# Weight tiles given up one at a time, and a longer warm-up, in a projection and attention kernel

## The chip, the core and the metric

The kernel runs on one core of a Trainium2 chip. The metric is device time in microseconds (us). The kernel before was run three times: 1155.35, 1155.54 and 1156.7 us, median 1155.54 us.

## What is computed

One layer with a normalisation, a projection to q, k, v and a gate, a two-dimensional neighbourhood attention, an output projection with a residual, and a last normalisation. Sizes: 2048 tokens (32 rows of 64 columns), model width 1024, 16 heads of 64; each query sees 8 rows by 16 columns of keys. Everything is float32.

```python
h = rmsnorm(x, norm_0)                      # (2048, 1024)
q, k, v, gate = split(h @ w_in_0, 4)        # w_in_0: (1024, 4096)
s = q k^T / 8 + rpb bias, masked to the 8 x 16 neighbourhood
o = softmax(s) v                            # per head
y = x + (o * silu(gate)) @ w_out_0          # w_out_0: (1024, 1024)
out = rmsnorm(y, norm_f)
```

## The kernel before

**Products in three terms.** To keep float32 accuracy, both operands of a projection are split into a high part of type fp32r and a low rest. Each product is three matmuls: high x high, high x low, low x high. ScalarE (ACT) makes the high part by a copy that rounds (`wh` at L197, `hh` at L175). VectorE (DVE) or GpSimd (POOL) makes the low part by a subtraction (`wl` at L198, `hl` at L176). Which of the two engines makes `wl` goes by the parity of weight unit and part, and POOL is used only after the second half-stage has begun (`state["half"] > 0`).

**Units and halves.** The input projection has 16 weight units of 256 columns: four each of q, k, v and gate. The tokens come in four groups of 512, two of them per phase `ph`. `halves` (L230 to L238) is the list of half-stages, each one kind of unit with one token group: first k, then q with token group 0, the same with group 1, then v with both groups, the gate with both, then the next heads. A q, k or gate half (`group`, L378) has two output groups `a`, each with eight steps `k` of three matmuls (L386, L388, L390), so 48 matmuls. A v half calls `group_v` (L394) four times, each eight steps of L402, L404, L406. The very first half is different: `first_groups` (L417) works on both output groups at once, step by step, with matmuls L425, L426 and L427.

**Items.** `items` is the list of all operands in the order of first use: ("w", (unit, phase), part) for a quarter of a weight unit, ("x", part, group) for the inputs, and squares and statistics for the normalisation. `load_item` (L133) issues the load of one on the SyncE queue (SP); `use_item` (L164) splits it. `consume` takes the next item if `may_use` allows it; it is called at fixed places between matmuls, and `need` forces it. So the program's order on every engine follows from when `may_use` first says yes. At least 32 items, and always five beyond the last used, are loaded ahead; raw tiles are few (pool `raw`, 6), so a load can also wait on SP until an earlier raw tile has been split.

**Weight tiles.** Split weights lie in the pool `wp` (10 buffers, so five pairs of `wh` and `wl`). A pair holds two of the four parts of a q, k or gate unit (four steps), or one part of two v units together (two steps). `may_use` (L272) counts the pairs that are live, and allows a new one up to five. A pair counts as live until the last half-stage of its unit is over (`last_use`, compared with `done_halves`).

**Around it.** After a group its PSUM bank is emptied by `evac` (L348) with DVE, ACT and POOL work, and the results are stored by SP. From half-stage 9 on, attention is interleaved with the projections: `normalise` (L562, POOL scales the exponentials `x`), `turns` (L579, transposes on PE), `scores` (L536) and `values` (L603), fed by a credit of projection matmuls; `feed` may run on a little if an item has just been used (`calm`). At the end `outputs` (L726) interleaves the output projection. All engines work in program order, SP's queue too.

**The start.** SP issues the load of `g0`, then in order: part 0 of the first weights, x parts 0 and 1, weight part 1, x parts 2 and 3, and so on. TensorE (PE) runs ten matmuls on a zero tile (L779, L780) ahead of the first real product.

Of the kernel before, what the change touches and what calls it, by code (L numbers as in the profile page):

```python
# [10 lines left out]
F32 = mybir.dt.float32  # L11
# [3 lines left out]
AF = mybir.ActivationFunctionType  # L15
OP = mybir.AluOpType
# [5 lines left out]
NK = D // 128  # L22
# [45 lines left out]
def build(ctx, tc, x, xt, wg, rpb, w_out, n0, nf, masks, out):  # L68
    nc = tc.nc
# [58 lines left out]
    hh, hl = {}, {}  # L128
    rb = {}
    raws, wh, wl, asked_at = {}, {}, {}, {}  # L130
    woh, wol = {}, {}

    def load_item(it):  # L133
        kind, a, b = it
        if kind in "trz":
            return
        if kind == "x" and b == 0:
            t = vp([128, 4, 128], F32, "land").rearrange("p g d -> p (g d)") if a < 6 else sp([128, 512], F32, "land")
        elif kind == "x" and b == 1 and a >= 4:
            t = kp([128, 960], F32, "land")[:, :512]  # L140
        elif it in items[12:16]:
            t = qp([128, 512], F32, "land")
        else:
            t = raw([128, 512], F32, "raw")
        raws[it] = t
        asked_at[it] = clock[0]
        if kind in "xs":
            nc.sync.dma_start(t, xt[a * 128:(a + 1) * 128, b * 512:(b + 1) * 512])
        elif kind == "w":
            u = a[0]  # L150
            nc.sync.dma_start(t.rearrange("p (k c) -> p k c", c=256), wg[u, :, 2 * b:2 * b + 2, :])
        else:
            nc.sync.dma_start(t, w_out[a * 128:(a + 1) * 128, b * 512:(b + 1) * 512])

# [9 lines left out]
    def use_item(it):  # L164
        kind, a, b = it
        state["event"] = clock[0]
        if kind == "t":
            return stats(b)
        if kind == "r":
            return spread_rstd(b)  # L170
        t = raws.pop(it)
        if kind == "x":
            h, l = xs([128, 512], F32R, "hh"), xs([128, 512], F32R, "hl")
            hh[a, b], hl[a, b] = h, l
            nc.scalar.activation(h, t, AF.Copy, scale=g0[:, a:a + 1])  # L175
            nc.vector.scalar_tensor_tensor(l, t, g0[:, a:a + 1], h.bitcast(F32), op0=OP.mult, op1=OP.subtract)  # L176
            if b < 2:
                raws["z", a, b] = t
        elif kind in "sz":
            square(a, t, b)  # L180
        elif kind == "w":
            t = t.rearrange("p (k c) -> p k c", c=256)
            u, ph = a
            if KINDS["v"] <= u < KINDS["g"]:
                a = u // 2 * 2, ph
                if u % 2 == 0:
                    wh[a, b] = wp([128, 2, 512], F32R, "wh")
                    wl[a, b] = wp([128, 2, 512], F32R, "wl")
                s = slice(u % 2 * 256, u % 2 * 256 + 256)
                h, l = wh[a, b][:, :, s], wl[a, b][:, :, s]  # L190
            else:
                if b % 2 == 0:
                    wh[a, b // 2] = wp([128, 4, 256], F32R, "wh")
                    wl[a, b // 2] = wp([128, 4, 256], F32R, "wl")
                s = slice(b % 2 * 2, b % 2 * 2 + 2)
                h, l = wh[a, b // 2][:, s], wl[a, b // 2][:, s]
            nc.scalar.activation(h, t, AF.Copy)  # L197
            (nc.gpsimd if (b + u) % 2 and state["half"] > 0 else nc.vector).tensor_tensor(l, t, h.bitcast(F32), OP.subtract)  # L198
        else:
            h, l = xs([128, 512], F32R, "woh"), xs([128, 512], F32R, "wol")  # L200
            woh[a, b], wol[a, b] = h, l
            nc.scalar.activation(h, t, AF.Copy)
            (nc.gpsimd if b else nc.vector).tensor_tensor(l, t, h.bitcast(F32), OP.subtract)
# [3 lines left out]
    def stats(c):  # L207
        acc = accs[c % 2]
        p = bank(16, "prt")
        for i in range(4):  # L210
            nc.tensor.matmul(p[:, i:i + 1], acc[:, i * 128:(i + 1) * 128], ones[:, :1], start=True, stop=True)
        m = tiny.tile([128, 8], F32, name="m")[:, :4]
        nc.vector.tensor_scalar(m, p[:, :4], 1.0 / D, EPS, op0=OP.mult, op1=OP.add)
        rsqrt(rt[:, 4 * c:4 * c + 4], m, 4)
        dg = dgs[c] = ev([128, 512], F32, "dg")
        for i in range(4):
            nc.vector.tensor_scalar(dg[:, i * 128:(i + 1) * 128], ident, rt[:, 4 * c + i:4 * c + i + 1], None,
                                    op0=OP.mult)

    def spread_rstd(c):  # L220
        p = bank(512, "prb")
        nc.tensor.matmul(p, ones, dgs.pop(c), start=True, stop=True)
        rb[c] = rbp([128, 512], F32, "rb")
        nc.scalar.activation(rb[c], p, AF.Copy)
# [14 lines left out]
    last_use = {}  # L239
# [10 lines left out]
    items, seen = [], set()  # L250
    for n, (k, j, ph, c) in enumerate(halves):
        a = (KINDS[k] + j, ph)
# [14 lines left out]
    items += [("o", a, b) for b in range(2) for a in range(NK)]  # L267
    AHEAD = 5
    clock = [0.0]
    state = dict(used=0, loaded=0, half=-1, done_halves=0, event=0.0)  # L270

    def may_use(it):  # L272
        kind, a, b = it
        d = state["done_halves"]
        if kind == "w":
            def tiles_(a, b):
                return (a[0] // 2 * 2, a[1], b) if KINDS["v"] <= a[0] < KINDS["g"] else (*a, b // 2)
            live = {tiles_(*i[1:]) for i in items[:state["used"]] if i[0] == "w" and last_use["w", i[1]] >= d}
            return len(live | {tiles_(a, b)}) <= 5
        if kind == "x":  # L280
            return sum(last_use["x", i] >= d for i in {i[2] for i in items[:state["used"]] if i[0] == "x"} - {b}) < 2
        if kind == "o":
            return last_use["x", 2 + b] < d
        return True
# [93 lines left out]
    def group(w, a, c, n):  # L378
        p = bank(512, "pp")
        cols = slice(a * 128, a * 128 + 128)  # L380
        for k in range(NK):
            if k in (3, 6) or n < 4:
                consume(1)
            need(("w", w, k // 2))
            need(("x", k, c))
            nc.tensor.matmul(p, wh[w, k // 4][:, k % 4, cols], hh[k, c], start=(k == 0), stop=False)  # L386
            yield 1
            nc.tensor.matmul(p, wh[w, k // 4][:, k % 4, cols], hl[k, c], start=False, stop=False)  # L388
            yield 1
            nc.tensor.matmul(p, wl[w, k // 4][:, k % 4, cols], hh[k, c], start=False, stop=(k == NK - 1))  # L390
            yield 1
        return p

    def group_v(w, t):  # L394
        c, o = divmod(t, 4)
        o = slice(o * 128, o * 128 + 128)
        p = bank(512, "pv")
        for k in range(NK):
            for u in range(2):
                need(("w", (w[0] + u, w[1]), k // 2))  # L400
            h, l = wh[w, k // 2][:, k % 2], wl[w, k // 2][:, k % 2]
            nc.tensor.matmul(p, hh[k, c][:, o], h, start=(k == 0), stop=False)  # L402
            yield 1
            nc.tensor.matmul(p, hh[k, c][:, o], l, start=False, stop=False)  # L404
            yield 1
            nc.tensor.matmul(p, hl[k, c][:, o], h, start=False, stop=(k == NK - 1))  # L406
            yield 1
            if k in (2, 5):
                consume(1)
        v = ev([128, 512], F32, "v")  # L410
        u = (w[0] - KINDS["v"]) // 2
        nc.scalar.activation(v, p, AF.Copy, scale=rt[:, t:t + 1])
        dst = vd[u].rearrange("h r c g d -> g (r c) h d")[t // 2, t % 2 * 128:t % 2 * 128 + 128]
        written.add(("v", u, t))
        store(("v", u, t), 8, lambda: nc.sync.dma_start(dst, v.rearrange("p (h d) -> p h d", h=4)))

    def first_groups(w):  # L417
        ps = [bank(512, "pp") for _ in range(2)]
        for k in range(NK):
            need(("x", k, 0))  # L420
            need(("w", w, k // 2))
            for a, p in enumerate(ps):
                cols = slice(a * 128, a * 128 + 128)
                h, l = wh[w, k // 4][:, k % 4, cols], wl[w, k // 4][:, k % 4, cols]
                nc.tensor.matmul(p, h, hh[k, 0], start=(k == 0), stop=False)  # L425
                nc.tensor.matmul(p, h, hl[k, 0], start=False, stop=False)  # L426
                nc.tensor.matmul(p, l, hh[k, 0], start=False, stop=(k == NK - 1))  # L427
        return ps

    def projections():  # L430
# [345 lines left out]
    z = ev([128, 512], BF16, "z")  # L776
    nc.gpsimd.memset(z, 0.0)
    zp = bank(512, "zp")
    for _ in range(10):  # L779
        nc.tensor.matmul(zp, z[:, :128], z, start=True, stop=True)  # L780

    amount = [96.0] * 16 + [(14 * 192 - 48 - 16 * 96) / 36] * 36 + [29.0] * 5 + [46.0] * 4 + [48.0] * (N + 1 - 61)
# [69 lines left out]
    for i in range(N + 1):  # L852
        a = amount[i]
# [52 lines left out]
```

## Time and profile before

| what | us |
|---|---|
| median of three runs | 1155.54 |
| the profiled execution | 1155.26 |
| its span, first to last instruction | 1153.5 |
| PE busy in the span | 1125.1 (98%) |
| DVE, ACT, POOL busy | 572.6, 467.5, 383.7 |
| projection matmuls L386, L388, L390, busy together | 885.5 |

A row of the timeline has start, duration, engine, line, operation, output and input tiles, and in brackets the idle time ahead of it and what ended it. A matmul's duration includes its way through the array, so consecutive starts, and not durations, give the pace. A row of the waits gives total, number and longest. A row of the windows gives, after the stretch and its length, the busy time of PE, of PE's weight loads, DVE, ACT and POOL with the number of instructions, then the granted PE clock, the DMA engines' share and GB/s.

### The profile page before, as it was taken

The page shows a single profiled execution, that of the slowest core. Times are in us where ns is not written, and L with a number is a line of the kernel's source. Part 1 is how long each engine was busy: PE and PEld are TensorE (multiplying, and loading weights), DVE is VectorE, ACT ScalarE, POOL GpSimd, SP SyncE. Part 2 cuts the span into 40 slices and gives each one's busy share as a digit, 9 for nine tenths or more (in the row PEclk, how much of TensorE's full clock was granted, in tenths as well). Part 3 has the DMA queues.
Part 4 walks back from the last instruction along what each step waited for, and adds up shares of the span by engine and source line. Part 5 has one row for each costly group of instructions (what it writes and reads, how often), then busy time and mean ns, then how long its engine had stood idle before and what let it go on. Part 6 is the DMA issues. An engine that isn't in the chain of part 4 may idle for free.

```text
span 1153.5 us, 21778 instructions
## 1 busy us (share of the span) xinstructions
PE 1125.1 (98%) x7858; PEld 916.4 (79%) x7858; DVE 572.6 (50%) x1453; ACT 467.5 (41%) x1190; POOL 383.7 (33%) x461
## 2 busy tenths in 40 slices
PE   8989999999999999999999999999999999999997
PEld 6868888888788888878887788888778777788875
DVE  6620554441244564126565455346555756566544
ACT  8222344232333444234444454344444544444322
POOL 1210442432232143314443544225533553233300
PEclk9999999999999999999999999999999999999999
DMA  7453867564554678457686787658877975865352
GB/s 244 126 160 109 270 213 219 162 225 110 154 183 145 214 222 240 118 165 195 224 245 198 207 250 222 208 163 230 235 230 210 281 230 188 255 194 189 104 174 73
DMA packets 139755, 224.45 MB, mean 195 GB/s; under 512 B 11776, under 2 KB 56320, under 8 KB 139648
## 3 DMA queue, kind: packets, MB, share of 16 engines
q1 hardware_dynamic: 139648, 223.06, 63.7%
q8 instruction: 62, 1.02, 0.4%
q14 instruction: 45, 0.37, 0.1%
HBM read 155.91 MB, written 67.11 MB: 193 GB/s over the span
## 4 chain that ended last, share of the span: by engine, by line
PE 58%; DMA 6%; DVE 3%; issue 3%; POOL 3%; ACT 1%; SPq 0%; DVEq 0%; POOLq 0%; ACTq 0%
PE pp L390 9%; PE pp L386 8%; PE pp L388 8%; PE o L617 6%; PE s L549 5%; PE po L763 4%; PE po L765 4%; PE po L761 4%; PE ph L572 3%; PE pv L404 3%; PE pv L402 3%; PE pv L406 3%; POOL x L567 1%; DMA ograw<-ogd 1%; DMA ogd<-og 1%
## 5 line engine op out<-in xcount | busy, mean ns | idle before, releaser
L390 PE MATMUL pp<-hh,wl 128*128 128x512 f32 x752 | 296.3, 394 | 2.0 <-POOL wl L198 2.0
L386 PE MATMUL pp<-hh,wh 128*128 128x512 f32 x752 | 295.3, 393 | 0.0
L388 PE MATMUL pp<-hl,wh 128*128 128x512 f32 x752 | 293.9, 391 | 0.0
L567 POOL TENSOR_SCALAR x<-x,st 128x360 f32<-128x360 f32 (+5 forms) x256 | 154.6, 623 | 250.7 <-DVE st L565 226.4
L559 ACT ACTIVATE x<-x,st 128x360 f32<-128x360 f32 (+5 forms) x256 | 151.8, 594 | 49.4 <-DVE st L556 49.3
L390 PEld LDWEIGHTS pp<-hh,wl 128*128 128x128 f32 x752 | 141.1, 188 | 33.4 <-POOL wl L198 2.9
L388 PEld LDWEIGHTS pp<-hl,wh 128*128 128x128 f32 x752 | 141.2, 188 | 30.5 <-issue 0.7
L386 PEld LDWEIGHTS pp<-hh,wh 128*128 128x128 f32 x752 | 141.2, 188 | 29.5 <-issue 0.5
L597 DVE COPY pta<-ph 128x384 f32<-128x384 f32 (+3 forms) x128 | 61.3, 516 | 165.8 <-PE ph L572 165.7
L198 POOL TENSOR_TENSOR wl<-raw,wh 128x512 fp32r<-128x512 f32 x60 | 83.3, 1393 | 161.6 <-ACT wh L197 155.2
L556 DVE CUSTOM_DVE_ANT_0 x<-s,em 128x360 f32<-128x360 f32 (+5 forms) x256 | 123.9, 539 | 7.3 <-PE s L549 5.3
L198 DVE TENSOR_TENSOR wl<-raw,wh 128x512 fp32r<-128x512 f32 x64 | 61.4, 969 | 93.9 <-ACT wh L197 92.6
L596 ACT ACTIVATE pta<-ph 96x256 f32<-96x256 f32 (+1 forms) x224 | 59.2, 333 | 118.7 <-PE ph L572 118.7
L402 PE MATMUL pv<-wh,hh 128*128 128x512 f32 x256 | 100.9, 394 | 3.5 <-ACT wh L197 3.5
L761 PE MATMUL po<-woh,gh 128*128 128x512 f32 x256 | 100.4, 392 | 2.1 <-ACT gh L671 2.0
L404 PE MATMUL pv<-wl,hh 128*128 128x512 f32 x256 | 101.4, 396 | 1.0 <-DVE wl L198 1.0
L763 PE MATMUL po<-woh,gl 128*128 128x512 f32 x256 | 100.4, 392 | 1.6 <-DVE gl L672 1.6
L765 PE MATMUL po<-wol,gh 128*128 128x512 f32 x256 | 100.9, 394 | 0.0
L406 PE MATMUL pv<-wh,hl 128*128 128x512 f32 x256 | 100.4, 392 | 0.0
L617 PEld LDWEIGHTS o<-pta,vt 96*64 96x64 f32 (+2 forms) x1792 | 83.8, 137 | 16.4 <-issue 11.0
L549 PE MATMUL s<-kt,qt 64*128 64x360 f32 (+5 forms) x768 | 93.1, 356 | 2.2 <-DVE pta L597 1.9
L531 POOL TENSOR_TENSOR em<-e,mk 128x360 f32<-128x360 f32 (+5 forms) x75 | 65.0, 869 | 89.9 <-DVE st L556 80.4
(85 smaller groups left out, 1373.9 us busy)
## 6 DMA issues: line engine op xcount, KB each, us to landing
raw<-in_wg_dram SPq DMA_DIRECT2D x124, 256.0 KB
vt<-vd SPq DMA_DIRECT2D x64, 192.0 KB
raw<-in_xt_dram SPq DMA_DIRECT2D x36, 256.0 KB
e<-in_rpb_dram SPq DMA_DIRECT2D x36, 240.0 KB
k_hi<-hi SPq DMA_DIRECT2D x32, 256.0 KB
k_lo<-lo SPq DMA_DIRECT2D x32, 256.0 KB
q_hi<-hi SPq DMA_DIRECT2D x32, 256.0 KB
q_lo<-lo SPq DMA_DIRECT2D x32, 256.0 KB
```

Source lines behind the costliest of these rows:

```text
L198: (nc.gpsimd if (b + u) % 2 and state["half"] > 0 else nc.vector).tensor_tensor(l, t, h.bitcast(F32), OP.subtract)
L386: nc.tensor.matmul(p, wh[w, k // 4][:, k % 4, cols], hh[k, c], start=(k == 0), stop=False)
L388: nc.tensor.matmul(p, wh[w, k // 4][:, k % 4, cols], hl[k, c], start=False, stop=False)
L390: nc.tensor.matmul(p, wl[w, k // 4][:, k % 4, cols], hh[k, c], start=False, stop=(k == NK - 1))
L404: nc.tensor.matmul(p, hh[k, c][:, o], l, start=False, stop=False)
L549: nc.tensor.matmul(pst[s], qq[a, qs], kk[a, :r1 - r0, c0:c1], start=(m == 0), stop=(m == 2))
L559: nc.scalar.activation(X[i, C][s], X[i, C][s], AF.Exp, bias=st[:, s:s + 1], scale=-1.0, accum_out=st[:, 2 + s:3 + s])
L567: nc.gpsimd.tensor_scalar(X[i, C][s], X[i, C][s], st[:, 4 + s:5 + s], 0.5, op0=OP.mult, op1=OP.mult)
L617: nc.tensor.matmul(o[s * 64:s * 64 + 64, C * 128 + q0:C * 128 + q0 + nq], vt[C][:k, g - g0_, s * 64:s * 64 + 64], t[:k, at:at + nq], start ...
L761: nc.tensor.matmul(p, gh[:, i], woh[i, j], start=(i == 0), stop=False)
L763: nc.tensor.matmul(p, gl[:, i], woh[i, j], start=False, stop=False)
L765: nc.tensor.matmul(p, gh[:, i], wol[i, j], start=False, stop=(i == NK - 1))
```

## The change

Three things are changed.

1. A weight pair stops counting as live when the program has written the last matmul that reads it, and not when its unit's last half-stage is over: `group` adds the pair to a set `freed` at steps 3 and 7 of the second output group of the unit's last half, `group_v` at every odd step of the last call in it, and `may_use` takes the set away from the live pairs.
2. 21 warming matmuls instead of ten.
3. In the first half, the three kinds of products go kind by kind: both output groups high x high, both high x low, both low x high. The first weight part is loaded as two halves, the second of them issued behind x part 0, and split in two as well, the second half behind x part 0's split.

```diff
+    second = []
...
         if kind in "xs":
             nc.sync.dma_start(t, xt[a * 128:(a + 1) * 128, b * 512:(b + 1) * 512])
+            if it == items[1]:
+                nc.sync.dma_start(raws[items[0]][:, 256:], wg[items[0][1][0], :, 1, :])
         elif kind == "w":
             u = a[0]
-            nc.sync.dma_start(t.rearrange("p (k c) -> p k c", c=256), wg[u, :, 2 * b:2 * b + 2, :])
+            if it == items[0]:
+                nc.sync.dma_start(t[:, :256], wg[u, :, 0, :])
+            else:
+                nc.sync.dma_start(t.rearrange("p (k c) -> p k c", c=256), wg[u, :, 2 * b:2 * b + 2, :])
...
+            if it == items[1]:
+                second.pop()()
...
-            nc.scalar.activation(h, t, AF.Copy)
-            (nc.gpsimd if (b + u) % 2 and state["half"] > 0 else nc.vector).tensor_tensor(l, t, h.bitcast(F32), OP.subtract)
+
+            def part(s, e):
+                nc.scalar.activation(h[:, s], t[:, s], AF.Copy)
+                e.tensor_tensor(l[:, s], t[:, s], h[:, s].bitcast(F32), OP.subtract)
+
+            if it == items[0]:
+                part(slice(0, 1), nc.vector)
+                second.append(lambda: part(slice(1, 2), nc.vector))
+            else:
+                part(slice(0, 2), nc.gpsimd if (b + u) % 2 and state["half"] > 0 else nc.vector)
...
+    freed = set()
...
-            live = {tiles_(*i[1:]) for i in items[:state["used"]] if i[0] == "w" and last_use["w", i[1]] >= d}
+            live = {tiles_(*i[1:]) for i in items[:state["used"]] if i[0] == "w" and last_use["w", i[1]] >= d} - freed
...
             nc.tensor.matmul(p, wl[w, k // 4][:, k % 4, cols], hh[k, c], start=False, stop=(k == NK - 1))
+            if k % 4 == 3 and a == 1 and n == last_use["w", w]:
+                freed.add((*w, k // 4))
...
             nc.tensor.matmul(p, hl[k, c][:, o], h, start=False, stop=(k == NK - 1))
+            if k % 2 and t % 4 == 3 and state["half"] == last_use["w", w]:
+                freed.add((*w, k // 2))
...
-            for a, p in enumerate(ps):
-                cols = slice(a * 128, a * 128 + 128)
-                h, l = wh[w, k // 4][:, k % 4, cols], wl[w, k // 4][:, k % 4, cols]
-                nc.tensor.matmul(p, h, hh[k, 0], start=(k == 0), stop=False)
-                nc.tensor.matmul(p, h, hl[k, 0], start=False, stop=False)
-                nc.tensor.matmul(p, l, hh[k, 0], start=False, stop=(k == NK - 1))
+            for m in range(3):
+                for a, p in enumerate(ps):
+                    cols = slice(a * 128, a * 128 + 128)
+                    t = (wl if m == 2 else wh)[w, k // 4][:, k % 4, cols]
+                    nc.tensor.matmul(p, t, (hl if m == 1 else hh)[k, 0], start=(k == 0 and m == 0),
+                                     stop=(k == NK - 1 and m == 2))
...
-    for _ in range(10):
+    for _ in range(21):
         nc.tensor.matmul(zp, z[:, :128], z, start=True, stop=True)
```

## The prediction

> **What bounds the kernel now.** I read the page first, then who waited for whom on TensorE, then the timeline at those places.
>
> ```profile
> span 1153.5 us, 21778 instructions
> PE 1125.1 (98%) x7858; PEld 916.4 (79%) x7858; DVE 572.6 (50%) x1453; ACT 467.5 (41%) x1190; POOL 383.7 (33%) x461
> PE pv L402 <- ACT wh L197: 3.5, 1, 3.5
> PE ph L572 <- POOL x L567: 3.2, 12, 0.4
> PE pp L425 <- ACT hh L175: 2.3, 1, 2.3
> PE pp L390 <- POOL wl L198: 2.0, 2, 1.0
> ...
> PE pv L404 <- DVE wl L198: 1.0, 1, 1.0
> ...
> PE pp L426 <- DVE hl L176: 0.3, 1, 0.3
> ```
>
> PE is busy 98% of the span, no other engine over 50%. So the time is PE's work at PE's pace, plus the few places where PE stands still or runs slowly. The number and kinds of real products do not change here, so only those places can move. Three kinds concern split weights or the start: L425 (2.3 us), L402 with L404 (4.5 us, one place), and L390 (2.0 us, two places).
>
> The pace, and the two slow places:
>
> ```profile
> 7.91 0.50 PE L425 MATMUL pp<-hh,wh 128*128 128x512 f32 x1 [2.27 <-ACT hh L175]
> ...
> 20.87 0.39 PE L386 MATMUL pp<-hh,wh 128*128 128x512 f32 x1
> ...
> 21.55 0.39 PE L386 MATMUL pp<-hh,wh 128*128 128x512 f32 x1
> 61.10 0.39 PE L406 MATMUL pv<-wh,hl 128*128 128x512 f32 x1
> ...
> 67.41 0.63 PE L402 MATMUL pv<-wh,hh 128*128 128x512 f32 x1
> 67.84 0.63 PE L404 MATMUL pv<-wl,hh 128*128 128x512 f32 x1
> ...
> 70.09 0.39 PE L404 MATMUL pv<-wl,hh 128*128 128x512 f32 x1
> 8.00:9.00 1.00, 0.72 (x2) 0.40 (x3) 1.00 (x2) 1.00 (x2) 0.00 (x0) 0.64 1.04 381
> 11.00:12.00 1.00, 1.00 (x4) 0.83 (x3) 1.00 (x3) 0.95 (x3) 0.00 (x0) 0.66 1.05 391
> ```
>
> Three matmuls take 21.55 - 20.87 = 0.68 us, so 0.227 us each at the full clock. From 67.41 to 67.84 it is 0.43: the granted clock is at half after an idle stretch. At the start it falls at about 8.3 us (0.64 over the slice 8 to 9) and is back at about 11.3 (0.66 over 11 to 12).
>
> **The start: 21 warming matmuls, order by kind, half loads.** The first 48 real products run from 7.91 to 20.87, 12.96 us, where 48 x 0.227 = 10.90 would do: 2.06 us lost, nearly all to the half clock.
>
> ```profile
> 1.83 3.81 PE L780 MATMUL zp<-z 128*128 128x512 bf16 x10 [1.83 <-POOL z L777]
> 4.37 0.15 PEld L780 LDWEIGHTS <-z 128*128 128x128 bf16 x1 [0.28 <-issue]
> 4.79 0.35 PEld L780 LDWEIGHTS <-z 128*128 128x128 bf16 x2 [0.28 <-issue]
> 8.42 0.63 ACT L197 ACTIVATE wh<-raw 128x512 fp32r<-128x512 f32 x1
> ...
> 10.44 0.63 ACT L197 ACTIVATE wh<-raw 128x512 fp32r<-128x512 f32 x1
> ```
>
> The weight loads of the warming matmuls are 0.43 us apart up to 4.79; the two at 4.79 lie within 0.35 us, so the second came 0.35 - 0.15 = 0.20 after the first. The clock was thus granted at about 4.8 us, lay unused from 5.64, and was taken back at 8.3. With 21, seven cold steps lead to 4.8 and fourteen more at about 0.214 (half of 0.427, an estimate) end at about 7.8. The first x part is split by 7.91 at the latest, so PE goes over into real products without a gap and keeps the clock. The eleven added matmuls cost nothing as long as PE would only wait; if that cover is gone, 0.1 to 1.6 us (below). Ordering by kind puts two products ahead of the first that needs `hl`; the wait of L426, 0.3 us, stood at that place, I keep 0.2. ACT delivers two steps in 10.44 - 8.42 = 2.02 us, PE consumes them in 12 x 0.227 = 2.72, so the extra load and the two half splits are hidden behind PE after the first step; the smaller first load can bring x sooner, but PE is then still warming, so that earns at most 0.1. New end of the first half: 7.85 + 10.90 + 0.2 = 18.95, **gain 1.9 us**. Bounds: 2.1 if nothing is left over, and below:
>
> Nothing says that the grant comes at 4.8 in every execution. If it came as late as the other edge shown, 8.3, the 21 would take 15 cold steps of 0.427 and 6 warm ones, ending at about 9.5; the first half would end at 9.5 + 10.9 = 20.4 and the gain be 0.4 us. That is the lower bound. [...]
>
> **The stall at 61 us: weight pairs given up one by one.** From 61.10 to 70.09 there are 11 steps, which take 8.99 us and should take 11 x 0.227 = 2.50. So this one place costs **6.49 us**: 4.5 idle, the rest half clock.
>
> ```profile
> 54.25 1.23 ACT L197 ACTIVATE wh<-raw 128x512 fp32r<-128x512 f32 x2 [2.89 <-DMA raw<-in_wg_dram]
> ...
> 63.76 0.61 ACT L197 ACTIVATE wh<-raw 128x512 fp32r<-128x512 f32 x1
> 48.25 1.98 SPq L151 DMA_DIRECT2D raw<-in_wg_dram  x3
> 53.72 0.33 SPq L151 DMA_DIRECT2D raw<-in_wg_dram  x1
> 55.55 1.28 POOL L198 TENSOR_TENSOR wl<-raw,wh 128x512 fp32r<-128x512 f32 x1 [4.76 <-ACT wh L197]
> ```
>
> The first two v units need four pairs. In q's last half q still holds two and v three, and a sixth is refused. So the split of v's last part (steps 6 and 7) was written only after the last q group, and stood on ACT behind the whole emptying of four banks, up to 63.76. In the changed program q's first pair is given up at step 3 of q's last output group. In the built order the split of the two quarters stands 13 and 19 products earlier, ahead of that emptying. All times here in the old frame: 61.10 is v's 18th product, so PE passes that step 3 some 30 products earlier, by 54.3. The loads of the two quarters were the last of the three issued from 48.25 to 50.23, and the one at 53.72. The slowest load near here, issued at 48.25, was used at 54.25, 6.0 us later; this gives at the latest 56.2 and 59.7. ACT is free from 55.48, and a split takes it 0.61. So `wh` is ready by 56.8 and 60.3 at worst, `wl` at most 1.3 us later: 58.1 and 61.6. PE wants them at 61.33 (step 6). If the second load takes half as long as the slowest (an estimate), there are 2.7 us to spare; at the worst 0.3 us are missing. The bank emptying moves behind at most one late load; its banks are wanted again only after groups of 24 x 0.227 = 5.4 us. I take **6.5 us**; bounds 0.3 us less if the worst load is late, 6.5 less if it doesn't work.
>
> **The gate after v: 2 x 1.0 us.** Here the reason is the same:
>
> ```profile
> 307.87 2.02 POOL L567 TENSOR_SCALAR x<-x,st 128x264 f32<-128x264 f32 x4 [31.86 <-DVE st L565]
> 309.86 2.52 POOL L198 TENSOR_TENSOR wl<-raw,wh 128x512 fp32r<-128x512 f32 x2
> 309.77 0.39 PE L388 MATMUL pp<-hl,wh 128*128 128x512 f32 x1
> 311.18 0.50 PE L390 MATMUL pp<-hh,wl 128*128 128x512 f32 x1 [1.02 <-POOL wl L198]
> ...
> 312.47 0.39 PE L388 MATMUL pp<-hl,wh 128*128 128x512 f32 x1
> 514.26 0.50 PE L390 MATMUL pp<-hh,wl 128*128 128x512 f32 x1 [1.02 <-POOL wl L198]
> ```
>
> The gate's third and fourth quarters need the pair of v's part 0, which was given up only when v was over. They are split when v is over; POOL has first to scale four `x` (2.02 us), and `wl` is late at step 6. From 309.77 to 312.47 six steps take 2.70 instead of 1.36: 1.34 us. The row at 514.26 shows the same wait, so 2.7 together. In the built order these splits stand 15 products, 3.4 us, earlier, ahead of POOL's `x`. That exceeds the delay, so **2.7 us** go; bounds 0 to 2.7.
>
> **Everything else that moves.** All other weight splits stand 6 to 18 products earlier (a few 30 to 46, past an attention block), with the loads that follow them; from the output weights on, the order is the same. A split waits on ACT for the matmul written just ahead of it; what stands behind it there needs later matmuls anyway, so this wait costs nothing. Attention blocks shift by at most a dozen products, with equal work. In three short attention intervals (22, 29, 32) a POOL split newly stands ahead of the scaling of `x`. I cost this at 0; the waits of L572 in the first fence show that the margin is small, bounded by 3 x 1.26 (two POOL splits take 2.52 above):
>
> ```profile
> 960.00:962.00 2.00, 1.64 (x18) 1.41 (x18) 0.82 (x2) 0.89 (x4) 0.42 (x1) 0.65 0.88 326
> 962.00:964.00 2.00, 2.00 (x16) 1.54 (x14) 1.34 (x5) 0.64 (x2) 0.00 (x0) 0.50 0.27 104
> ```
>
> The last two rows are a third half-clock stretch, by short attention waits: 1.4 + 2 us at half the clock, so up to 1.7 us lost. Moving everything by 11 us may keep it, drop it or make another: 1.7 either way.
>
> **Sum.** 1.9 + 6.5 + 2.7 = 11.1 us. The profiled execution took 1155.26 (1.76 around its span), so 1144.2; the median of the runs is 0.28 higher, so **1144.4 us**.
>
> **The rivals.**
>
> - *The stall moves* (9%). The last v quarters come just too late, because the second load can't be issued until its raw tile is split (53.72). The rest remains: 1144.4 + 6.5 = 1150.9. For it: ACT waited 2.89 us for a load there; against: at the worst 0.3 us are missing.
> - *The grant comes late* (8%): the start gains 0.4 instead of 1.9, so 1145.9, as worked out above from the two edges shown. For it: nothing ties the grant to the kernel's start; against: the one execution shown had it at 4.8. [...]
> - *Attention pays* (5%). The three POOL splits delay `turns` by 1.26 us each: 1148.2.
> - *Slower* (4%). SP works in order, and more than a dozen weight loads now stand ahead of attention's `vt` loads and of stores, each waiting for a raw tile (the first row is of 560 to 900 us):
>
> ```profile
> SPq L151 <- POOL wl L198: 6.8, 4, 3.5
> 306.84 0.55 SPq L507 DMA_DIRECT2D vt<-vd  x1
> 323.39 1.33 PE L617 MATMUL o<-pta,vt 96*64 96x128 f32 x24
> ```
>
>  A wait of 3.5 us at the head of SP, if it reached PE, would cost 3.5 per attention pair; from four such pairs on the gain is gone, and at five it is 1144.4 + 17.5 = 1161.9. Against it: a `vt` issued at 306.84 is used at 323.39 or later, a lead of over 16 us.
> - *Only the warm-up works* (4%): pairs come free earlier in the program, but PE waits at the same places: 1155.5 - 1.9 = 1153.6.
>
> **How the numbers follow.** The forecast has 70%. Its own range is 1142.5 (1.7 for the half clock, 0.2 at the start) to about 1146. The range of 8 in 10 reaches on over the late grant and attention's waits, to 1149; left out are 9 + 4 + 4 = 17%. A change of 0.2%, 2.3 us, is about what a measurement of this kernel can tell from none. Forecast, moved stall, late grant and attention lie under 1153.2: 92% faster; only the warm-up: 4% the same; 4% slower.
>
> **What would show it.** Right: in the profile after, no wait of L402 for `wh` and no slice under full clock between 60 and 70 us; the waits of L390 gone; the warming matmuls end at about 7.8 and the first L386 starts near 19.0. Wrong: a wait of `pv` for `wl` or of ACT for a weight load at 50 to 60 us (the stall moved); a gap or half clock between warming and the first products; more than 3.2 us of L572 waiting for `x`; `o` waiting for `vt`.

## The result, and the profile after

The median of four runs of the changed kernel is 1143.94 us (1142.6 to 1145.46), beside 1156.1 us for four runs of the kernel before. The ratio is 0.9898, 95% interval 0.9883 to 0.9913, so 10.0 to 13.5 us less; predicted was 1144.4. The profiled execution of after took 1145.46 us, the slowest of its four, against 1155.26 for that of before: 9.8 us less.

The first view is the head of the page after and its two longest waits (total us, number, longest):

```profile
span 1143.7 us, 21798 instructions
PE 1124.3 (98%) x7869; PEld 917.7 (80%) x7869; DVE 568.9 (50%) x1454; ACT 469.4 (41%) x1191; POOL 383.9 (34%) x461
PE po L782 <- ACT gh L692: 4.8, 2, 4.3
PE ph L593 <- POOL x L588: 2.8, 10, 0.4
```

The lines that the prediction was about are gone: no product of `pv` waits for `wh` or `wl` (before: 3.5 and 1.0 us), and no `pp` waits for POOL's `wl` (before 2.0). The scaling of `x` costs 2.8, not more than the 3.2 of before. New at the top is a wait of an output product for `gh`, 4.8 us, which stood in no step of the prediction. Eleven matmuls more, each with its weight load, are the warming; one instruction more on DVE and one on ACT are the halved first split.

Next, the same stretch of the windows in both kernels, before first, then after:

```profile
60.00:70.00 10.00, 5.57 (x17) 3.98 (x16) 4.99 (x5) 3.83 (x7) 3.32 (x3) 0.83 0.91 275
```

```profile
60.00:70.00 10.00, 10.00 (x46) 8.28 (x45) 4.66 (x6) 4.64 (x8) 3.90 (x3) 1.00 0.89 271
```

PE has 46 matmuls where it had 17, at a granted clock of 1.00 instead of 0.83.

The timeline of after, at the start and where v begins:

```profile
1.83 7.66 PE L801 MATMUL zp<-z 128*128 128x512 bf16 x21 [1.83 <-POOL z L798]
6.15 0.72 ACT L181 ACTIVATE hh<-land,g 128x512 fp32r<-128x512 f32 x1 [2.17 <-DMA land<-in_xt_dram]
9.13 0.82 PE L447 MATMUL pp<-hh,wh 128*128 128x512 f32 x2
20.23 0.39 PE L403 MATMUL pp<-hh,wh 128*128 128x512 f32 x1
54.81 2.66 ACT L207 ACTIVATE wh<-raw 128x512 fp32r<-128x512 f32 x4 [4.01 <-DMA raw<-in_wg_dram]
56.15 0.80 PE L421 MATMUL pv<-wh,hh 128*128 128x512 f32 x1
57.37 0.58 ACT L240 ACTIVATE rb<-prb 128x512 f32<-128x512 f32 x1
57.49 1.71 DVE L208 TENSOR_TENSOR wl<-raw,wh 128x512 fp32r<-128x512 f32 x1 [1.33 <-ACT wh L207]
```

The last four of v's eight splits now stand in one row on ACT, from 54.81, and the bank emptying (`rb`) comes behind them. The first real product starts at 9.13, behind the warming matmuls, which the prediction had end at about 7.8. Meanwhile x part 0 is split by 6.15 + 0.72 = 6.87, an us earlier than in before, and lies there waiting for PE.

Five places that both kernels pass in the same order say where the 9.8 us of the profiled executions went (us from the span's start, by the first matmul of each):

| place | before | after | difference |
|---|---|---|---|
| first half over | 20.87 | 20.23 | 0.64 |
| v begins | 56.79 | 56.15 | 0.64 |
| the gate behind the second v pair begins | 305.47 | 298.27 | 7.20 |
| the gate behind the third begins | 508.55 | 500.00 | 8.55 |
| last output product | 1145.23 | 1135.27 | 9.96 |

So the start gave 0.64, the stall 6.56, the first gate wait 1.35, and all that follows 1.41, in which the second gate wait (1.34) lies.

The last stretch holds more than that, and it cancels: without that gate wait it is 0.07 us shorter. The half-clock stretch of before at 961 is gone, but after has two others: one from 895.3 to 898.7 and one from 973.8 on, behind a wait for `gh` (each of them is the 0.97 in one row of 50 us below; before has 1.00, 1.00 and 0.97 in the same three). Timeline, windows and queue waits of after:

```profile
973.41 1.15 ACT L692 ACTIVATE gh<-ograw 128x512 fp32r<-128x512 f32 x2 [7.60 <-DMA ograw<-ogd]
974.09 0.80 PE L782 MATMUL po<-woh,gh 128*128 128x512 f32 x1 [4.33 <-ACT gh L692]
```

```profile
850.00:900.00 50.00, 48.81 (x436) 39.81 (x433) 33.36 (x87) 25.34 (x72) 14.61 (x22) 0.97 0.80 249
900.00:950.00 50.00, 48.77 (x425) 39.44 (x424) 33.28 (x82) 26.93 (x74) 29.96 (x33) 1.00 0.77 227
950.00:1000.00 50.00, 45.67 (x372) 36.78 (x371) 29.86 (x98) 21.50 (x62) 13.83 (x18) 0.97 0.71 220
974.00:975.00 1.00, 0.91 (x2) 0.47 (x3) 0.93 (x2) 0.56 (x2) 0.00 (x0) 0.50 1.05 350
```

```profile
SPq L680 <- DMA ogd<-og: 5.2, 1, 5.2
```

The first stretch follows a gap of 1.19 us on PE, which ends at 894.07. Before has the like gap ahead of the same products, 1.22 us up to 905.47, and keeps the full clock; from the end of the gap to the same product after it takes 1.56 us longer (4.81 instead of 3.25). At 974 PE stands for 4.33 us until ACT has split a tile of the attention's output, and resumes at half the clock. ACT waited for its load, and on SP's queue that load had waited 5.2 us for the store of the same data. In before's profile the store was waited for 2.5 us, and PE 1.70:

```profile
SPq L659 <- DMA ogd<-og: 2.5, 1, 2.5
984.87 0.49 PE L761 MATMUL po<-woh,gh 128*128 128x512 f32 x1 [1.70 <-ACT gh L671]
```

Shorter waits stand against this, among them those for `pta` and `gl` (1.9 and 1.6 us in before, 1.2 and 0.2 in after); the parts of this stretch were not all added up.

### The profile page after: what moved, and what is told of

It reads as the page before. It is cut to its first block, busy times and chain, and to the rows that moved or that the text cites. A ratio compares the mean times of both kernels' runs of the same rounds, so it can differ in the third digit from the quotient of the medians.

```text
span 1143.7 us, 21798 instructions
## 1 busy us (share of the span) xinstructions
PE 1124.3 (98%) x7869; PEld 917.7 (80%) x7869; DVE 568.9 (50%) x1454; ACT 469.4 (41%) x1191; POOL 383.9 (34%) x461
## 3 DMA queue, kind: packets, MB, share of 16 engines
q8 instruction: 62, 1.02, 0.4%
## 4 chain that ended last, share of the span: by engine, by line
PE 93%; DMA 2%; DVE 2%; POOL 1%; issue 1%; ACT 1%; DVEq 0%; SPq 0%; POOLq 0%; ACTq 0%
PE pp L407 15%; PE pp L405 15%; PE pp L403 15%; PE o L638 7%; PE s L570 6%; PE pv L423 5%; PE pv L425 5%; PE pv L421 5%; PE po L786 4%; PE po L784 4%; PE po L782 4%; PE ph L593 4%; PE pp L447 1%; POOL x L588 1%; DMA ograw<-ogd 1%
## 5 line engine op out<-in xcount | busy, mean ns | idle before, releaser
L407 PE MATMUL pp<-hh,wl 128*128 128x512 f32 x752 | 296.1, 394 | 0.0
L407 PEld LDWEIGHTS pp<-hh,wl 128*128 128x128 f32 x752 | 141.4, 188 | 30.3
L208 POOL TENSOR_TENSOR wl<-raw,wh 128x512 fp32r<-128x512 f32 x60 | 79.7, 1332 | 228.9 <-ACT wh L207 222.1
L552 POOL TENSOR_TENSOR em<-e,mk 128x360 f32<-128x360 f32 (+5 forms) x75 | 67.8, 905 | 102.5 <-DVE st L577 95.8
L208 DVE TENSOR_TENSOR wl<-raw,wh 128x512 fp32r<-128x512 f32 (+1 forms) x65 | 60.1, 928 | 79.5 <-ACT wh L207 78.3
L638 PEld LDWEIGHTS o<-pta,vt 96*64 96x64 f32 (+2 forms) x1792 | 84.3, 138 | 16.2 <-issue 11.3
L638 PE MATMUL o<-pta,vt 128*64 128x128 f32 (+4 forms) x1792 | 93.2, 255 | 0.5 <-DVE pta L618 0.5
```

The source lines that it names most:

```text
L638: nc.tensor.matmul(o[s * 64:s * 64 + 64, C * 128 + q0:C * 128 + q0 + nq], vt[C][:k, g - g0_, s * 64:s * 64 + 64], t[:k, at:at + nq], start ...
```

## The experiments

The theory is the prediction's: the stall of L402 and the waits of L390 come from where the splits stand on ACT and POOL, and giving pairs up early moves them ahead of what delayed them; the start gains what the clock grant allows. The main rivals: the gain is the warm-up's, or the moved splits pay elsewhere. Ratios are to the kernel before, with 95% intervals; its median stood at 1155.23, 1155.58 and 1155.31 us beside the three groups of experiments. The kernel line numbers shift by a few from kernel to kernel.

### e1_freed_only: only the giving up

Before, with the `freed` set in `may_use`, `group` and `group_v`, and nothing else of the change:

```diff
+    freed = set()
-            live = {... if i[0] == "w" and last_use["w", i[1]] >= d}
+            live = {... if i[0] == "w" and last_use["w", i[1]] >= d} - freed
+            if k % 4 == 3 and a == 1 and n == last_use["w", w]:
+                freed.add((*w, k // 4))
+            if k % 2 and t % 4 == 3 and state["half"] == last_use["w", w]:
+                freed.add((*w, k // 2))
```

> The kernel before with weight pairs given up at their last product, and nothing else: ten warming matmuls, old order and one whole first weight load. My theory: the stall at 61 us (6.5 us) and the two waits of L390 (2.7 us) go, the start stays, so 9.2 us less, ratio about 0.992; in the profile the first matmul of the second half stage (L386 of before) starts at 20.9 us as before. Rival (the start carries the gain, the pairs only move waits): less than 4 us gained, with new waits for weights elsewhere. Rival (the parts help each other): under 8 us, because the late start brings back part of the stall.

Measured: 1144.51 us, ratio 0.9915 (0.9903 to 0.9927), 9.8 us less. Its timeline and its waits:

```profile
20.90 0.39 PE L387 MATMUL pp<-hh,wh 128*128 128x512 f32 x1
```

```profile
PE po L766 <- ACT gh L676: 2.3, 2, 2.1
PE pp L430 <- ACT hh L175: 2.1, 1, 2.1
```

The first half ends where before's does (20.87), and the waits of `pv` and L391 are gone. The gates begin at 299.02 and 500.78: 6.45 and 7.77 earlier. Nearly the whole gain is this part's.

### e2_start_only: only the start

After, without the two `freed.add`:

```diff
-            if k % 4 == 3 and a == 1 and n == last_use["w", w]:
-                freed.add((*w, k // 4))
-            if k % 2 and t % 4 == 3 and state["half"] == last_use["w", w]:
-                freed.add((*w, k // 2))
```

> The changed kernel without giving up pairs: 21 warming matmuls, products by kind and the halved first load stay. My theory: 0.4 to 1.9 us gained by when the clock is granted, ratio 0.9984 to 0.9997; the wait of the v group for its weights near 60 us (3.5 and 1.0 us) and both 1.0 us waits for the gate's low parts stand as before, a little earlier. Rival (the start carries the gain): 4 us or more.

Measured: 1154.21 us over 12 runs, ratio 0.9996 (0.9986 to 1.0007): nothing that can be told from none. In the profile the start works and its gain is lost 45 us later. Timeline, waits and windows:

```profile
1.83 6.79 PE L797 MATMUL zp<-z 128*128 128x512 bf16 x21 [1.83 <-POOL z L794]
19.38 0.39 PE L403 MATMUL pp<-hh,wh 128*128 128x512 f32 x1
```

```profile
PE pv L419 <- ACT wh L207: 3.7, 1, 3.7
PE pv L421 <- DVE wl L208: 1.0, 1, 1.0
```

```profile
64.00:65.00 1.00, 0.25 (x1) 0.00 (x0) 1.00 (x2) 0.21 (x1) 0.52 (x1) 0.55 0.94 227
67.00:68.00 1.00, 1.00 (x4) 0.75 (x3) 0.00 (x0) 0.22 (x1) 0.00 (x0) 0.50 1.05 299
70.00:71.00 1.00, 1.00 (x4) 0.76 (x3) 0.00 (x0) 0.00 (x0) 0.34 (x1) 0.53 1.16 256
```

The first half ends 1.49 us earlier and v begins 1.49 earlier, at 55.30; the gate begins at 305.40, only 0.07 earlier. The wait of 3.7 + 1.0 is much that of before (3.5 + 1.0): it moved forward with PE and ends 1.21 earlier. But the half clock now lasts from 64.1 to 70.9, 6.8 us, where before's lasted from 66.3 to 69.7, 3.4 us. The two rows of before:

```profile
66.00:67.00 1.00, 0.58 (x2) 0.51 (x3) 0.87 (x2) 0.00 (x0) 0.00 (x0) 0.65 0.99 260
69.00:70.00 1.00, 1.00 (x4) 0.77 (x4) 0.00 (x0) 1.00 (x2) 0.00 (x0) 0.65 0.91 307
```

So in this execution the early start was lost to a longer half clock behind the stall, and only 0.3 us of it to a longer wait.

### e3_freed_qkg and e4_freed_v: the giving up in two parts

Before with `freed`, once added to only in `group` (q, k, gate), once only in `group_v`:

```diff
+            if k % 4 == 3 and a == 1 and n == last_use["w", w]:
+                freed.add((*w, k // 4))
```

> The kernel before, with pairs given up early only in the groups of q, k and gate. My theory: the stall at 61 us goes and both waits of L390 of 1.0 us stay: 6.5 us less, ratio about 0.9944. Rival (a general relief of ACT, POOL and the loads): about half of the 9.2 us with each half of the edit, and no clean assignment of waits.

```diff
+            if k % 2 and t % 4 == 3 and state["half"] == last_use["w", w]:
+                freed.add((*w, k // 2))
```

> The kernel before, with pairs given up early only in the groups of v. My theory: the stall at 61 us stays whole (waits of 3.5 and 1.0 us and half clock to 69.9) and both waits of L390 go: 2.7 us less, ratio about 0.9977. Rival (a general relief): about half of 9.2 us.

Measured: e3 1146.44 us, 0.9929 (0.9915 to 0.9943), 8.2 us less (6.6 to 9.8); e4 1154.17 us, 0.9986 (0.9976 to 0.9995), 1.6 less (0.6 to 2.8). The windows and waits of e3, then the waits of e4:

```profile
60.00:70.00 10.00, 10.00 (x46) 8.29 (x45) 5.54 (x6) 4.42 (x8) 4.08 (x3) 1.00 0.87 284
```

```profile
PE pp L391 <- POOL wl L198: 2.0, 2, 1.0
```

```profile
PE pv L403 <- ACT wh L197: 3.5, 1, 3.5
```

The two places part cleanly: `group`'s pairs carry the stall of v, `group_v`'s pairs the waits of the gate. By the places, e3 has gained 6.35 us at the third gate (502.20 against 508.55), e4 1.51 (507.04), of which 0.16 is its start. The medians lie 1.7 above (e3) and 1.1 below (e4) the 6.5 and 2.7 of the working; both intervals take in or nearly touch them, and the stretch behind the third gate, whose length varies from run to run (633.7 to 636.7 us in the twelve profiles that feed as before does there), can make that difference.

### e11_split_before_emptying: what the stall's cause is

Is it that the pair is free, or where the split stands on ACT? Before, without `freed`; only, at the end of q's last half, the two v quarters are split ahead of the last bank emptying instead of behind it:

```diff
                     if n == 3 and a == 1:
+                        state["done_halves"] = 4
+                        consume(2)
                         flush(1)
```

> The kernel before, except that the two last v quarters are split right after the last q product, ahead of the emptying of the four banks. No pair is given up before its unit is over. My theory (the stall's cause is their place behind that emptying on ACT, not the scarcity of pairs in itself): the stall at 61 us goes whole, 6.4 us or, with the second window at half clock, up to 7.9; ratio about 0.9944; both waits of L390 stay. Rival (the pair must be free at step 3, half a group earlier): the wait of pv for wh or wl shrinks by less than half.

Measured: 1149.78 us, 0.9951 (0.9938 to 0.9965), 5.7 us less (4.0 to 7.2). Windows, timeline and waits:

```profile
60.00:70.00 10.00, 10.00 (x45) 8.27 (x45) 6.03 (x8) 4.79 (x9) 3.90 (x3) 1.00 0.79 234
```

```profile
55.65 1.94 ACT L197 ACTIVATE wh<-raw 128x512 fp32r<-128x512 f32 x3 [2.74 <-DMA raw<-in_wg_dram]
59.22 0.63 ACT L197 ACTIVATE wh<-raw 128x512 fp32r<-128x512 f32 x1 [1.62 <-DMA raw<-in_wg_dram]
59.75 0.58 ACT L224 ACTIVATE rb<-prb 128x512 f32<-128x512 f32 x1
```

```profile
PE pp L390 <- POOL wl L198: 2.0, 2, 1.0
```

The stall is gone with no pair given up any earlier than the end of q's matmuls: the cause is the splits' place in the program's order, behind the emptying. From v's begin to the gate behind the second v pair it takes 248.68 us in before and 242.15 in e11, as in after (242.12), e1 and e3 (both 242.19): the whole 6.5. The experiment moves the splits on ACT, DVE and POOL together; that ACT's place was the one that cost most is read from before's waits (3.5 us for ACT, then 1.0 for DVE). The median shows 5.7; in the profile the first half ended 1.22 later than before's (22.09; the clock came at about 14, with products 0.43 us apart until then), and whether it did in the other runs is not shown. The last load is late here (ACT waits 1.62 for it) and still not too late. The gate's waits stay, as they must.

### e5, e6, e7, e8: how many warming matmuls

Before with 21 (e5); after with 10 (e6), 14 (e7) and 40 (e8) instead of 21. Each is one number:

```diff
-    for _ in range(10):
+    for _ in range(21):
```

> The kernel before with 21 warming matmuls, and nothing else. With g the moment when the clock is granted, the first real product stands at 6.31 + 0.5 (g - 1.83) us (cold steps of 0.427, warm ones of 0.2135, from 1.83 us on): 7.8 for a grant at 4.8, 9.4 for one at 8.0. My theory: this alone holds the clock, so the second half stage's first matmul (L386 of before) comes 10.9 to 11.2 us after the first product, 18.9 to 20.4 in all, with no wait of its own for the new order or the halved load. Rival (the order by kind and the halved load carry the gain of the start): 20.5 or later, or half clock after the first product.

```diff
-    for _ in range(21):
+    for _ in range(10):
```

> The changed kernel with ten warming matmuls instead of 21. In the changed kernel's profile the first x part is split at 6.9 us, an us earlier than before. [...] Theory 2 (the prediction's: the clock is lost again after a pause, as in the kernel before, and 21 are needed): half clock from about 8 to 11.5, end of the first half at 19.6 or later, no better than the changed kernel.

```diff
-    for _ in range(21):
+    for _ in range(14):
```

> The changed kernel with 14 warming matmuls. By the times seen so far (grants between 4.6 and 7.5 us) the 14 end between 6.3 and 7.7, about when the first x part is split (6.9). Both theories: clock kept, first product at 6.9 to 7.7, end of the first half at 18.0 to 18.8, so 0.9 us or more before that of 21 at the same grant; ratio to before about 0.989. Rival (fewer than 21 lose the clock): half clock after the first product, end at 19.6 or later.

```diff
-    for _ in range(21):
+    for _ in range(40):
```

> The changed kernel with 40 warming matmuls: the price of one that isn't needed. First real product at 10.37 + 0.5 (g - 1.83) us, 11.9 to 13.4; end of the first half 22.8 to 24.4, 4.1 us behind that of 21 at the same grant, if each further warming matmul costs 0.2135 us. Rival (PE would have waited for operands anyway, so warming is free): under 21 us.

The start in the timelines of e5, e6, e7 and e8, in this order:

```profile
1.83 6.51 PE L780 MATMUL zp<-z 128*128 128x512 bf16 x21 [1.83 <-POOL z L777]
```

```profile
6.97 1.22 PE L447 MATMUL pp<-hh,wh 128*128 128x512 f32 x2 [0.70 <-ACT hh L181]
9.70 1.05 PE L447 MATMUL pp<-hh,wh 128*128 128x512 f32 x2
11.18 0.63 PE L447 MATMUL pp<-hh,wl 128*128 128x512 f32 x2
```

```profile
1.83 4.94 PE L801 MATMUL zp<-z 128*128 128x512 bf16 x14 [1.83 <-POOL z L798]
7.30 0.73 PE L447 MATMUL pp<-hh,wh 128*128 128x512 f32 x2 [0.54 <-ACT hh L181]
18.65 0.39 PE L403 MATMUL pp<-hh,wh 128*128 128x512 f32 x1
```

```profile
1.83 10.89 PE L801 MATMUL zp<-z 128*128 128x512 bf16 x40 [1.83 <-POOL z L798]
12.37 0.81 PE L447 MATMUL pp<-hh,wh 128*128 128x512 f32 x2
```

- e5, one run: 1152.01 us beside 1155.58. The clock is kept and the first half ends at 19.44, 1.43 earlier; the gate begins at 304.99, only 0.48 earlier: as in e2, the half clock behind the stall lasts 6.8 us (63.5 to 70.4) and takes the rest back. The rest of what this run lies below before stands behind the third gate (633.92 us there, 636.68 in before's profile), where the edit changes nothing.
- e6: 1144.36 us (1141.19 to 1145.1), 0.9898 (0.9883 to 0.9914). Its profile does not show a clock that was granted and lost again: it was not granted in the ten at all, which took 4.45 us, where before's took 3.81. The first real products take their steps at half clock, 0.43 us each, until about 10.7. The first half ends at 19.83, so the numbers expected for a lost clock (19.6 or later, no better than the changed kernel) came out by another way, and the time is that of the changed kernel with 21. So in the changed kernel no gain of 21 over ten is shown; what e6 keeps of the start, the order by kind and the halved load, brings the end of the first half 1.04 us forward against before, although the clock comes so late.
- e7: 1142.65 us (1141.47 to 1143.4), 0.9887 (0.9871 to 0.9904). Fourteen end at 6.8, PE stands 0.54 us for x and keeps the clock (products 0.23 us apart from 8.65 on); the first half ends at 18.65, 1.6 earlier than in after's profile. The early split of x, done at 7.25 here, is now used.
- e8, one run: 1148.04 us. The first half ends at 23.48, 4.10 behind that of e2, where the clock was granted at about the same time (6.2 and 6.1, by the lengths of the warming blocks): 19 warming matmuls more at 0.216 us each.

### e9 and e10: 14 warming matmuls with less feed, and the wait for gh

After with 14 warming matmuls and less credit for projection and output matmuls in five attention intervals, 26 (e9) or 23 (e10) instead of 29, so that PE comes to the product that needs `gh` up to 15 or 30 matmuls later:

```diff
-    for _ in range(21):
+    for _ in range(14):
...
-... + [29.0] * 5 + ...
+... + [26.0] * 5 + ...
```

> The changed kernel with 14 warming matmuls, and with 26 instead of 29 projection matmuls fed in each of the five intervals before the second token block's output tiles: 15 output matmuls (3.4 us) stay back for the moment when PE waits for the first tile of that block (L782 waiting for gh: 2.8 us in the kernel with 14 warming matmuls, 4.8 in the changed one). Theory: that wait goes, 1 to 2.5 us gained against 14 warming matmuls alone, ratio to before about 0.987. Rival: those 15 matmuls covered attention's own waits (L593 for x, L570 for pta), which grow by as much, and the time stays at a ratio of 0.9887.

> As the run before, with 23 instead of 29: 30 output matmuls (6.8 us) stay back. Theory: no more gain than with 26, as 2.8 us is all there is to hide, and attention's waits begin to grow: ratio 0.987 to 0.989. Rival: the feed isn't what covers the wait, and the time is that of 14 warming matmuls alone, with L782 still waiting 2 us or more.

Measured: e9 1140.75 us (1140.09 to 1141.17), 0.9877 (0.9864 to 0.989); e10 1142.55 us, 0.9895 (0.9878 to 0.9911). The waits of e9, then of e10:

```profile
SPq L680 <- DMA ogd<-og: 5.6, 1, 5.6
PE s L570 <- ACT pta L617: 2.4, 2, 2.1
PE po L782 <- ACT gh L692: 0.3, 1, 0.3
```

```profile
PE s L570 <- ACT pta L617: 3.7, 1, 3.7
```

In e9 the store of `og` is waited for even longer than in after (5.6 us, 5.2 there), and PE waits 0.3 for `gh` instead of 4.8; attention pays a part of it, 2.4 us in L570. In e10 attention pays 3.7 there, and the gain over 14 warming matmuls alone is gone. Against those alone (e7, 0.9887) the intervals of both overlap, so what the smaller feed is worth by itself is not shown.

### e12_after_again: the change once more

The changed kernel itself, beside e9 on the same chip:

> The changed kernel once more, beside the three others. Expected from its first runs: ratio 0.989 to 0.991, start of the second half stage between 19.0 and 20.5 us by when the clock is granted, and a wait of L782 for gh of 1.5 to 5 us that follows how long the store of og takes to land (5.2 us of waiting on the load queue in the changed kernel's profile, 2.5 in that of before).

Measured: 1143.86 us (1142.0 to 1146.98), 0.9907 (0.9892 to 0.9922). Timeline and waits:

```profile
1.83 7.07 PE L801 MATMUL zp<-z 128*128 128x512 bf16 x21 [1.83 <-POOL z L798]
```

```profile
PE po L782 <- ACT gh L692: 2.3, 2, 2.1
```

The median repeats to 0.1 us, the ratio less closely (0.9898 and 0.9907). The first half ends at 19.65, not 20.23, and `gh` costs 2.3, not 4.8: both vary with one and the same kernel. All of e9's runs lie below all of these: e9 as a whole, with 14 warming matmuls and the smaller feed, is faster than the changed kernel.

## Why the prediction was right, point by point

- **The stall, 6.5 us: right, mechanism and size.** 6.56 in after, 6.45 in e1 (both at the gate behind the second v pair), 6.35 in e3 (at the third gate). e11 shows the cause, the place behind the bank emptying. The margin was overrated. The step put the usual spare time at 2.7 us, up to v's step 6; in after the last `wl` is ready at 57.49 + 1.71 = 59.20, and PE reaches step 6 at 60.68: 1.5 us. ACT had waited 4.01 us for the first of these loads.
- **The gate waits, 2.7 us: right.** 1.35 in after, 1.35 in e4, 1.32 in e1 for the first; no wait of L407 (L390 of before) for `wl` is left at either. e3 and e4 show that they belong to `group_v`.
- **The start, 1.9 us: mis-sized, and the mechanism right in part.** The profiled execution gained 0.64. That 21 keep the clock is right (e5, after: no half clock follows them; in e5 products stand 0.227 us apart from 9.00 on). The failing step is "seven cold steps lead to 4.8 and fourteen more at about 0.214 end at about 7.8": the grant came at 7.8, so the block ran on to the first product at 9.13, and the bound for that, 0.4 us, was the better guide for this execution. That 21 are needed at all is not borne out in the changed kernel: with ten (e6) the ratio is the same, 0.9898.
- **When the clock came.** The prediction has the clock back at 11.3 in before; by its own row, 0.66 from 11 to 12, it is 11.68, so the half clock lasts 3.4 us and not 3.0, which changes no term of the sum. The clock column stands at 1.00 ahead of the first grant even where the pace is half (e6: 1.00 in every slice from 4 to 10 us, with products 0.43 apart), so the grant has to be worked out. From the lengths of the warming blocks (cold steps of 0.427 us, as from 2.23 to 7.78 in after; warm ones of 0.2135, half of that, an estimate) the grant came at 4.6 to 5.5 us in e1, e3, e4, e5 and e7, at 6.1 to 6.7 in e2, e8, e10 and e12, at 7.2 in e9, at 7.8 in after, and in e6 and e11 not within their ten (by the pace of the products at about 10.7 and 14). So it varies from run to run, with 4.6 to 7.8 us for the same first instructions on PE; what it depends on is not shown.
- **What the start is worth.** Over the three profiles with 21 warming matmuls and the whole start of the change (after, e2, e12) the first half ends at 20.23, 19.38 and 19.65, mean 19.75; over five with the old start (before, e1, e3, e4, e11) at 20.87, 20.90, 20.98, 20.71 and 22.09, mean 21.1. So the start is worth about 1.4 us by the profiles, with a spread larger than itself (0.5 to 2.7 from pair to pair). By the times, after and e12 lie 11.8 and 10.7 us below before and e1, without the start, 9.8: 0.9 to 2.0 us.
- **The first load in two parts, at most 0.1 us: right only because 21 warming matmuls stand in its way.** In after x's split comes an us earlier (6.87 instead of 7.83), which PE can't use before 9.13. With 14 it can: the first half ends at 18.65 (e7) and 18.45 (e9).
- **The 0.2 us for `hl`: right in size by luck.** From 9.13 to 20.23 are 11.10 us, and 48 x 0.227 = 10.90. But no wait for `hl` stands among after's waits; the 0.2 lies in the first two products, 0.66 us up to the next pair at 9.79 instead of 0.45, and as much in e8 (12.37 to 13.01), with `hl` long there. What takes it is open.
- **Everything else at 0, by 1.7 either way: the balance right, the parts not foreseen.** The half clock at 961 went and another came at 895, 1.6 us, both as allowed for ("drop it or make another"). That the output product could wait 4.8 us for `gh` was not seen, though the row of 1.70 stood in before. Why the store of `og` lands later in some executions (waited for 2.5 us in before, 3.0 in e12, 5.2 in after, 5.6 in e9) stays open.
- **The rivals.** The moved stall didn't come (no ACT wait reached PE); the late grant did, in part, in the profiled execution; attention didn't pay (2.8 instead of 3.2); no product on PE waits for `vt`. Only the warm-up: e2 answers it, the whole start alone gives 0.5 us with an interval across zero.

**The sum.** By the ratio the kernels are 11.8 us apart (10.0 to 13.5), in e12 10.7. Stall 6.6, gates 2.7 and start 1.4 make 10.7; the remaining 1.1 of the first lies within its interval, and no experiment assigns it.

## What to carry to other kernels

Where an engine takes its work in the order written, as ACT did in e11, and makes operands for another, look not at whether a buffer is free but at what is written ahead of the instruction that makes them: two splits moved ahead of a bank emptying gave 5.7 of the 9.8 us that giving up each pair early gave, and in the profile the whole stall. A gain ahead of a stall can be lost at the stall, as in the profiles of e2 and e5, where the half clock behind it lasted 6.8 us instead of 3.4; so remove the stall first and judge the start after it. Size a warm-up by when the first operand arrives, and not longer: here 14 matmuls and ten did as well as 21, and 40 cost 0.22 us for each one more.

## What the runs showed of the hardware

- The same stall, 4.1 to 4.7 us idle, costs different amounts of time: 6.5 in before, but 6.5 + 1.49 - 0.07 = 7.9 in e2 and 6.5 + 1.43 - 0.48 = 7.4 in e5. Behind it the half clock lasted 3.4 us in before (66.3 to 69.7), and 6.8 in e2 (64.1 to 70.9) and e5 (63.5 to 70.4). It lasted 3.4 in before's start too, from 8.28 to 11.68 (0.64 in the slice from 8 to 9, 0.66 in that from 11 to 12), and in after from 895.3 to 898.7. What sets its length, and so why it lasted twice as long in e2 and e5, is not shown.
- Gaps of 0.5 to 2.3 us on PE kept the full clock in some places and were followed by half of it in others. 0.54 us in e7's start, 1.02 at before's gates, 1.70 at before's 984 and 1.22 at its 905 kept it. 2.27 in before's start (5.64 to 7.91) was followed by the half clock, and so was 1.19 in after at 894, ahead of the same products as the 1.22. What decides between them is not shown.
